# Level products of both head pairs in one run, a new order of the first loads, and three smaller moves

## The chip, the cores and the metric

The kernel runs on one core of a Trainium2 chip. The time is that of one execution on the device in microseconds (us), the median of several runs. One core has five engines with a queue of instructions each: TensorE (PE: matrix products; its weight loads are shown as PEld), VectorE (DVE), ScalarE (ACT), GpSimd (POOL) and SyncE (SP, which issues most loads). An engine works its queue in order; where an instruction needs something from another engine or from a DMA, it waits on a semaphore, and everything behind it waits too.

## The reference, cut to what matters

One layer of an encoder trunk with 512 rows (frames) of 1024 features, all float32:

```python
hn   = rmsnorm(x)
proj = hn @ w_in                      # fox q,k,v,f | hgrn q,f,i,g
A    = forgetting_attention(...)      # 8 heads of 64, causal softmax, bias F[t]-F[s]
B    = hgrn2_chunkwise(...)           # 4 heads, state 128x128, chunks of 64
x   += concat(A, B') @ w_out          # B' = rmsnorm(B) * silu(g)
x   += cross_attention(rmsnorm(x), rmsnorm(mem))   # 256 memory rows, 4 heads
x   += relu(rmsnorm(x) @ w1)**2 @ w2  # d_ff = 4096
out  = rmsnorm(x)
# inside hgrn2, for a chunk of 64 frames:
decay = exp(bcum[t] - bcum[s])        # for every feature d, s <= t
attn  = einsum('td,sd,tsd->ts', q, k, decay)
```

## The kernel before, in words

**Numbers.** Every product of projections is made with operands split into a high and a low part (fp32r), so one product of the reference is three on TensorE: high x high, high x low, low x high. `hn_hi`, `hn_lo` are the two parts of the normed input, `wh..` and `wl..` those of a weight panel. The high part is a copy on ScalarE (line 167), the low part a subtraction on VectorE (line 169), which needs the high part. A panel has 256 columns; number 11 has the halves `11a` and `11b` over K (the 1024 features that are summed over, in 8 chunks of 128).

**Order.** TensorE's instructions go in the order of the program text. The other engines' queues are ordered by a list scheduler with priorities when the kernel is built (`ahead(n)` shifts a priority, `tc.issue_after` and `tc.keep_in_program_order` bind one instruction behind others). `Fill` is a queue of generators of projection products: `fill.run(us)` takes steps from it until so many microseconds' worth have been issued. So TensorE has work between products whose operands are still being made.

**Start.** x is loaded by column blocks into `xt` (`load_x`): first columns 0 to 128 on SyncE's queue, then 128 to 256 and the next two blocks of 256 on ScalarE's, and the last on SyncE's behind the first weight panel, which is loaded in four parts of 256 KB (`load_next(4)`, `wr0a` twice and `wr0b` twice). `x_T(c)` transposes a chunk of 128 columns on TensorE into `xn`, `x_hi` and `x_lo` make `hn_hi`, `hn_lo` of it. Two accumulations `gf` (128 columns of the panel each) run over the eight chunks c, six products for each chunk, and `x_T(c + 2)` comes behind those of c. Before all of it, six products of zeros (`warm`) run.

**HGRN.** The decay between two frames in a chunk of 64 is split by levels: at level m = 1, 2, 4, .. 64 the frames are blocks of m, and the pairs in neighbouring blocks (odd block as t, even block as s) get their `attn` from one product of `mov` and `mix`. There are four heads in two head pairs (hp). For each level and each head pair: ScalarE copies `mix` from the scaled keys and queries; TensorE makes 16 small products of 64 x 64 into `lv` (8 of 128 x 128 at m = 64; line 670); VectorE copies them under a mask into `Ac` (`copy_predicated`, line 673); VectorE and GpSimd scale `sta` and `mov` (lines 693 and 694) by F, the decay to the edge of a block, and GpSimd brings F to the next level (line 696); then `fill.run(F2)`, 2.7 us of projections. The diagonal products `dg` (line 611), one for each of the four heads, with a `fill.run(F1)` of 1.6 us behind each, come ahead of the levels.

**Fox attention.** Units (head pair p, 128 rows tb, head j) are worked one behind another: bias, scores, a softmax (`mx` for the maximum, Exp, `dn` for the sum), and the transpose `pt` of the probabilities on TensorE, which is copied from PSUM into `pta`, `ptb` or `pts`, by ScalarE for j = 0 (line 910) and VectorE for j = 1 (line 912). Memory rows are transposed (`mnt`) in between, and split by ScalarE (`meh`) and VectorE (`mel`, line 365). Panels 11 and 12 (`wh11b`, `wl11b`, `wh12a`, ..) are split there too, for products that come later. `xq` and `k` operands (`q`, `kh`, `kl`) are made there.

**MLP.** It is computed in groups with sums of quadrants (a Strassen-like scheme): units of weights `whu`, `wlu` (up) and `whd`, `wld` (down); `prep` splits a unit's raw tile, `unit` calls `prep` for as many as four units ahead of use. `uU`, `uY` are products up, `c` and `h` are combined hidden parts, `hb` their high and low parts. A PSUM bank is free for the next product when VectorE or ScalarE has read it.

**Tail.** For each block of 128 rows, the squares of the last sum `acc` are added up in pieces (`squares`: ScalarE's Square with a sum, then `fe` adds the sum so far), GpSimd takes the power -1/2 (`fr`), and ScalarE and VectorE scale the rows (`fo`).

## Time and profile before

| what | value |
|---|---|
| median of 3 runs | 766.73 us (765.64 to 766.76) |
| the profiled execution | 765.97 us |
| its span, first to last instruction | 763.9 us |
| TensorE busy | 751.6 us (98%) |
| VectorE, ScalarE, GpSimd busy | 559.7, 427.1, 182.9 us |
| moved by DMA | 113.08 MB, 148 GB/s on average |

The span is shorter than the execution by 2.1 us, which lie around the first and the last instruction. In the rows below, a line of the timeline has the start, the duration, engine, line, what is written and read, the count, and in brackets the idle time ahead and what ended it; groups of equal instructions have one row. A line of the windows has the stretch, the sum, busy time and count by engine (PE, PEld, DVE, ACT, POOL, unless it is for certain instructions alone), TensorE's granted clock as a share of full speed, the share of the DMA engines' time and GB/s. A line of the waits has who waited for what: the total, the count and the longest.

### The profile page before, as it was taken

To read this page: it belongs to the slowest core of one execution; us is meant where nothing else is said; L and a number is where in the kernel's file an instruction comes from. 1 tells how busy PE (TensorE), PEld (TensorE's weight loads), DVE (VectorE), ACT (ScalarE), POOL (GpSimd) and SP (SyncE) were. 2 spreads that over 40 slices of the span, in tenths; PEclk is the share of its full clock that TensorE was granted. 3 is DMA by queue.
4 is the path that set the end of the run, shared out by engine and by line. 5 is a ranking of instruction groups with operands and counts; after the bars stand their busy time and mean duration, and the time that the engine had idled before them with its cause. 6 is when DMAs were issued, how large, how long until landed. Compare 5 with 4: busy or idle time off the path is not lost.

```text
span 763.9 us, 12648 instructions
## 1 busy us (share of the span) xinstructions
PE 751.6 (98%) x4844; PEld 665.8 (87%) x4844; DVE 559.7 (73%) x889; ACT 427.1 (56%) x718; POOL 182.9 (24%) x261
## 2 busy tenths in 40 slices
PE   8999999999999999999999999999999999999996
PEld 5889878978989988888888898999999999999985
DVE  4746766797677746645557789869797979897984
ACT  4655555676656533334445576656565757565743
POOL 7106343444343005510000111211212121211122
PEclk9999999999999999999999999999999999999998
DMA  7643322243444443221124498896979797978612
GB/s 225 216 114 86 111 82 57 84 111 85 142 161 137 131 150 111 87 79 56 56 83 137 83 295 171 231 253 161 249 165 241 183 268 164 280 148 213 161 47 110
DMA packets 84221, 113.08 MB, mean 148 GB/s; under 512 B 4881, under 2 KB 62778, under 8 KB 84162
## 3 DMA queue, kind: packets, MB, share of 16 engines
q1 hardware_dynamic: 70418, 74.77, 30.9%
q0 software_dynamic: 11568, 35.15, 22.6%
q10 hardware_dynamic: 2176, 2.36, 0.9%
q8 instruction: 38, 0.62, 0.3%
q14 instruction: 21, 0.17, 0.1%
HBM read 88.14 MB, written 4.21 MB: 121 GB/s over the span
## 4 chain that ended last, share of the span: by engine, by line
PE 90%; DVE 3%; DMA 2%; ACT 2%; issue 1%; POOL 1%; POOLq 0%; ACTq 0%; SPq 0%; DVEq 0%
PE uU L1394 4%; PE uU L1393 4%; PE uU L1395 4%; PE U L1495 3%; PE U L1496 3%; PE U L1497 3%; PE uY L1393 3%; PE uY L1395 3%; PE uY L1394 3%; PE xq L232 2%; PE xq L233 2%; PE xw L232 2%; PE xw L234 2%; PE xw L233 2%; PE xq L234 2%; PE wo L233 2%
## 5 line engine op out<-in xcount | busy, mean ns | idle before, releaser
L167 ACT ACTIVATE whd<-wq 128x1024 fp32r<-128x1024 f32 x39 | 41.3, 1058 | 31.3 <-PE U L1497 12.9
L169 DVE TENSOR_TENSOR wld<-wq,whd 128x1024 fp32r<-128x1024 f32 x39 | 47.6, 1220 | 7.1 <-ACT whd L167 7.1
L167 ACT ACTIVATE whu<-uq 128x1024 fp32r<-128x1024 f32 x28 | 29.7, 1062 | 33.0 <-PE uY L1394 14.3
L1395 PE MATMUL uU<-x2s,wlu 128*128 128x256 f32 x160 | 45.3, 283 | 0.0
L1393 PE MATMUL uU<-x2s,whu 128*128 128x256 f32 x160 | 45.2, 283 | 0.0
L1495 PE MATMUL U<-whd,hb 128*128 128x512 f32 x112 | 43.9, 392 | 0.0
L1496 PE MATMUL U<-wld,hb 128*128 128x512 f32 x112 | 43.9, 392 | 0.0
L1497 PE MATMUL U<-whd,hb 128*128 128x512 f32 x112 | 43.6, 389 | 0.0
L1250 POOL DMA_DIRECT2D uk<-us x8 | 7.2, 906 | 149.6 <-ACT acc L1114 85.7
L1467 DVE SCALAR_TENSOR_TENSOR acc<-U,r,acc 128x512 f32<-128x512 f32 x56 | 40.2, 744 | 1.8 <-PE U L1497 1.2
L169 DVE TENSOR_TENSOR wlu<-uq,whu 128x1024 fp32r<-128x1024 f32 x28 | 34.2, 1221 | 5.7 <-ACT whu L167 5.4
L1394 PE MATMUL uU<-x2a,whu 128*128 128x256 f32 x128 | 36.2, 283 | 0.0
L1394 PE MATMUL uY<-x2a,whu 128*128 128x256 f32 x128 | 36.2, 283 | 0.0
L1394 PE MATMUL uU<-x2b,whu 128*128 128x256 f32 x128 | 36.2, 283 | 0.0
L167 ACT ACTIVATE whu<-us 128x1024 fp32r<-128x1024 f32 x20 | 21.2, 1062 | 21.6 <-PE uU L1394 17.9
L169 DVE TENSOR_TENSOR wlu<-us,whu 128x1024 fp32r<-128x1024 f32 x20 | 24.4, 1221 | 10.8 <-ACT whu L167 10.8
L1393 PEld LDWEIGHTS uU<-x2s,whu 128*128 128x128 f32 x160 | 30.6, 191 | 0.8
L1395 PEld LDWEIGHTS uU<-x2s,wlu 128*128 128x128 f32 x160 | 30.6, 191 | 0.0
L889 ACT ACTIVATE bi<-bi,mx 128x128 f32<-128x128 f32 (+3 forms) x32 | 18.0, 561 | 20.5 <-DVE mx L887 20.2
L1250 POOL DMA_DIRECT2D wq<-in_w_dram x10 | 12.2, 1221 | 71.6 <-DMA wq<-in_w_dram 60.9
L872 POOL TENSOR_SCALAR bi<-nF,Ft 128x128 f32<-128x128 f32 (+3 forms) x32 | 21.5, 673 | 31.1 <-PE pt L899 17.1
L1393 PE MATMUL uY<-x2s,whu 128*128 128x256 f32 x96 | 27.3, 284 | 1.0 <-DVE c L1405 1.0
(961 smaller groups left out, 2809.1 us busy)
## 6 DMA issues: line engine op xcount, KB each, us to landing
wq<-in_w_dram SPq DMA_DIRECT2D x31, 512.0 KB, 6.0
uq<-in_w_dram SPq DMA_DIRECT2D x12, 512.0 KB, 4.7
us<-in_w_dram SPq DMA_DIRECT2D x12, 512.0 KB, 6.8
wq<-wq POOLq DMA_DIRECT2D x11, 512.0 KB, 6.4
wq<-in_w_dram POOLq DMA_DIRECT2D x10, 512.0 KB, 9.0
uk<-in_w_dram SPq DMA_DIRECT2D x8, 512.0 KB, 4.1
uk<-us POOLq DMA_DIRECT2D x8, 512.0 KB, 4.5
uq<-uk POOLq DMA_DIRECT2D x8, 512.0 KB, 6.1
```

What stands on the lines that cost most here:

```text
L167: ac.activation(hi, raw, AF.Copy)
L169: ve.tensor_tensor(lo, raw, f(hi), ALU.subtract)
L232: te.matmul(ps, wh, hi, start=n_ == 0, stop=False)
L233: te.matmul(ps, wh, lo, start=False, stop=False)
L234: te.matmul(ps, wl, hi, start=False, stop=n_ == KC - 1)
L1393: te.matmul(ps[:, i, :], whi[:, k, ws], xh, start=first_ and (k, i) == (0, 0), stop=False, skip_group_check=True)
L1394: te.matmul(ps[:, i, :], whi[:, k, ws], xl, start=False, stop=False, skip_group_check=True)
L1395: te.matmul(ps[:, i, :], wlo[:, k, ws], xh, start=False, stop=k == 3, skip_group_check=True)
L1467: ve.scalar_tensor_tensor(a, ps, r2[:, 0 if sign > 0 else 1, tb : tb + 1], a, op0=ALU.mult, op1=ALU.add)
L1495: te.matmul(ps, hi, whi[:, k, :], start=first_ and k == 0, stop=False, skip_group_check=True)
L1496: te.matmul(ps, hi, wlo[:, k, :], start=False, stop=False, skip_group_check=True)
L1497: te.matmul(ps, lo, whi[:, k, :], start=False, stop=k == 1, skip_group_check=True)
```

## The change

Five edits, which touch few instructions of TensorE.

1. *First loads and products.* SyncE now issues the columns of x from 256 on, between the parts of the first panel, and the first of these issues waits for a copy of one element on ScalarE (`xt<-ones`, behind ScalarE's table load), since it writes where the load writes. The first chunk's six products go high x high for both `gf`, then low weight, then `hn_lo`.
2. *Products in one run.* The `dg` products of a pair's two heads, and the `lv` products of both head pairs, follow each other, and the fill behind them is double. The scalings of `sta`, `mov` and F come, in the text, ahead of the copies under the mask.
3. *Two weights.* The split of the second half of panel 11 is put behind unit 3 of Fox attention, and the split of one MLP unit (u, 1, 6) behind the `hb` of part "6".
4. *Copies.* `pt` of the first head pair (p = 0) is copied by ScalarE for both heads.
5. *Last squares.* In the last block the last piece is squared on VectorE by one reduction that starts from the sum so far; the epsilon is added one step earlier.

```diff
@@ -152,7 +152,7 @@
     stream = []
-    state = {"used": 0, "then": None}
+    state, later = {"used": 0, "then": None}, []
     UW, UK = WT + FH, KC // 2
@@ -181,7 +181,9 @@
             for sl, src in spec:
-                nc.sync.dma_start(raw_[:, qs, sl], src[:, src_ks, :])
+                load = nc.sync.dma_start(raw_[:, qs, sl], src[:, src_ks, :])
+                if between is not None:
+                    tc.keep_in_program_order(load)
             if between is not None:
@@ -203,11 +205,14 @@
         while len(stream) < min(state["used"] + 2, len(specs)):
-            for split in load_next():
+            for half, split in enumerate(load_next()):
                 with ahead(PW), ExitStack() as order:
                         order.enter_context(tc.issue_after(ins))
-                    split()
+                    if (len(stream), half) == (12, 1):
+                        later.append(split)
+                    else:
+                        split()
         if state["used"] == len(specs) - 1:
@@ -222,16 +227,16 @@
-    def gemm_fm(ps, wt, col, ahi, alo, n=S, order=range(KC)):
+    def gemm_fm(ps, wt, col, ahi, alo, n=S, order=range(KC), begun=False):
             wh, wl = chunk(whi, k, sl), chunk(wlo, k, sl)
-            te.matmul(ps, wh, hi, start=n_ == 0, stop=False)
+            te.matmul(ps, wh, hi, start=n_ == 0 and not begun, stop=False)
             te.matmul(ps, wh, lo, start=False, stop=False)
-            te.matmul(ps, wl, hi, start=False, stop=n_ == KC - 1)
+            te.matmul(ps, wl, hi, start=False, stop=n_ == len(order) - 1)
             yield 3 * n / 2400
@@ -308,14 +313,19 @@
         gs = slice(g, g + n)
-        queue.dma_start(xt[:, :, gs], x[:, gs].rearrange("(t p) n -> p t n", p=P))
-
+        return queue.dma_start(xt[:, :, gs], x[:, gs].rearrange("(t p) n -> p t n", p=P))
+
+    ones = cp.tile([P, 1], F32, name="ones")
+    ve.memset(ones, 1.0)
     load_x(0, P, nc.sync)
     load_x(P, P)
-    for q in range(1, 3):
-        load_x(q * WT)
-    first = load_next(4)
-    load_x(3 * WT, queue=nc.sync)
+    tc.keep_in_program_order(ac.activation(xt[:, 0, WT : WT + 1], ones, AF.Copy))
+
+    def x_behind(part):
+        if part < 3:
+            tc.keep_in_program_order(load_x((part + 1) * WT, queue=nc.sync))
+
+    first = load_next(4, x_behind)
     rows = t2("rows", F32, (P,))[0:33, :]
@@ -330,8 +340,6 @@
     ve.memset(mhalf, -0.5)
-    ones = cp.tile([P, 1], F32, name="ones")
-    ve.memset(ones, 1.0)
@@ -444,7 +452,11 @@
         gfps = [mm(f"gf{i}") for i in range(2)]
-        gfg = [gemm_fm(gfps[i], wt0, i * P, hn_hi, hn_lo) for i in range(2)]
+        for part in ("hh", "lh", "hl"):
+            for i, ps in enumerate(gfps):
+                w, a = (wt0["hl".index(part[0])][0][:, 0, i * P : (i + 1) * P], (hn_hi, hn_lo)["hl".index(part[1])][:, 0, :])
+                te.matmul(ps, w, a, start=part == "hh", stop=False)
+        gfg = [gemm_fm(gfps[i], wt0, i * P, hn_hi, hn_lo, order=range(1, KC), begun=True) for i in range(2)]
         second = []
@@ -471,7 +483,7 @@
         for c in range(KC):
-            for g in gfg:
+            for g in gfg if c else ():
                 next(g)
@@ -611,7 +623,7 @@
             gp.tensor_tensor(qt_(h), qt_(h), Fg[hp][:, j, :], op=ALU.mult)
-            fill.run(F1)
+        fill.run(2 * F1)
@@ -655,8 +667,9 @@
             gate_rows()
+        lvs = []
         for hp in range(2):
-            F_, M_, S_ = Fg[hp], Mv[hp], Sa[hp]
+            M_ = Mv[hp]
             mix = t2(f"mix{hp}{m}", F32, (NT, P))
@@ -664,10 +677,21 @@
             ps = sc(f"lv{hp}{m}", (NT, 2, w))
+            lvs.append(ps)
             for c in range(NT):
                     te.matmul(ps[o : o + 2 * w, c].rearrange("p u (b m) -> p u b m", m=m), mix[:, c, o : o + 2 * w], rhs, start=True, stop=True)
+        for hp in range(2):
+            F_, ps = Fg[hp], lvs[hp]
+            for j in range(2):
+                h = 2 * hp + j
+                qv, kv, fv = halves(qt_(h), m), halves(kt_(h), m), halves(F_[:, j, :], m)
+                bshape = [P, S // (2 * m), m]
+                ve.tensor_tensor(qv[:, :, 1, :], qv[:, :, 1, :], fv[:, :, 0, 0:1].to_broadcast(bshape), ALU.mult)
+                (ve, gp)[j].tensor_tensor(kv[:, :, 0, :], kv[:, :, 0, :], fv[:, :, 1, 0:1].to_broadcast(bshape), op=ALU.mult)
+            fv = halves(F_.rearrange("p h t -> p (h t)"), m)
+            gp.tensor_tensor(fv[:, :, 0, 0:1], fv[:, :, 0, 0:1], fv[:, :, 1, 0:1], op=ALU.mult)
             if m < 64:
@@ -686,15 +710,7 @@
                     last_copy.append(ve.tensor_copy(A_[hi_, 4:8, lo_], ps[hi_, :, 1, :]).ins)
-            for j in range(2):
-                h = 2 * hp + j
-                qv, kv, fv = halves(qt_(h), m), halves(kt_(h), m), halves(F_[:, j, :], m)
-                bshape = [P, S // (2 * m), m]
-                ve.tensor_tensor(qv[:, :, 1, :], qv[:, :, 1, :], fv[:, :, 0, 0:1].to_broadcast(bshape), ALU.mult)
-                (ve, gp)[j].tensor_tensor(kv[:, :, 0, :], kv[:, :, 0, :], fv[:, :, 1, 0:1].to_broadcast(bshape), op=ALU.mult)
-            fv = halves(F_.rearrange("p h t -> p (h t)"), m)
-            gp.tensor_tensor(fv[:, :, 0, 0:1], fv[:, :, 0, 0:1], fv[:, :, 1, 0:1], op=ALU.mult)
-            fill.run(F2)
+        fill.run(2 * F2)
     fq, fk = {}, {}
@@ -861,7 +877,7 @@
     units = [(p, tb, j) for p in range(4) for tb in range(NT) for j in range(2)]
-    prob, probT, held_T = {}, {}, {}
+    prob, probT, held_T, ends = {}, {}, {}, {}
@@ -886,9 +902,9 @@
             den = sm(1, f"dn{h}{tb}")
-            ac.activation(b, b, AF.Exp, bias=mx, scale=-1.0, accum_out=den)
+            exp = ac.activation(b, b, AF.Exp, bias=mx, scale=-1.0, accum_out=den)
             ve.reciprocal(den, den)
-            ve.tensor_scalar(b, b, den, None, op0=ALU.mult)
+            ends[u] = exp.ins, ve.tensor_scalar(b, b, den, None, op0=ALU.mult).ins
@@ -906,7 +922,7 @@
                 probT[u] = held_T[p, tb % 2][:, j, (0 if tb else 3 * P) :][:, 0:n]
-            if j == 0:
+            if j == 0 or p == 0:
                 ac.activation(probT[u], pt[:, 0:n], AF.Copy)
@@ -957,6 +973,9 @@
                 fill.until("fv0")
+            if n == 4:
+                with ahead(PW), tc.issue_after(ends[units[3]][0]), tc.issue_after(ends[units[3]][1]):
+                    later.pop()()
             if n + 1 < len(units):
@@ -1279,7 +1298,7 @@
-    last_sum = {}
+    last_sum, hb_ins = {}, {}
@@ -1311,7 +1330,7 @@
         unit_ = new_parts([k, D // k], f"{kind}{g}{name}")
-        with ahead(PW):
+        with ahead(PW), tc.issue_after(hb_ins[0, "6"]) if (kind, g, name) == ("u", 1, "6") else nullcontext():
             split_of(unit_[0], unit_[1], raw.rearrange("p (k n) -> p k n", k=k))()
@@ -1323,7 +1342,8 @@
         kept = sum(k in units and keys.index(k) < keys.index(key) for k in last_keys)
-        while unit_q and kept + sum(k in units for k in keys[keys.index(key) :]) < 4:
+        room = 3 if key == ("u", 1, "2") else 4
+        while unit_q and kept + sum(k in units for k in keys[keys.index(key) :]) < room:
             prep(*unit_q.popleft())
@@ -1431,7 +1451,7 @@
         sign = -1.0 if name == "6" else 1.0
-        ac.activation(hb[:, 0], src, AF.Copy, scale=sign)
+        hb_ins[g, name] = ac.activation(hb[:, 0], src, AF.Copy, scale=sign).ins
         if name == "6":
@@ -1515,10 +1535,15 @@
             outs[tb] = k4([D], f"fo{tb}")
+        if last and tb == NT - 1:
+            a = acc[tb][:, cs]
+            tc.keep_in_program_order(ve.tensor_tensor_reduce(out=outs[tb][:, cs], in0=a, in1=a, scale=1.0 / D, scalar=sums[tb][-1], op0=ALU.mult, op1=ALU.add, accum_out=ms))
+            sums[tb].append(ms)
+            return
         ac.activation(outs[tb][:, cs], acc[tb][:, cs], AF.Square, scale=1.0 / 32.0, accum_out=ms)
             e = sm(1, f"fe{tb}{n}")
-            (ve if last else gp).tensor_scalar(e, ms, sums[tb][-1], EPS if last else 0.0, op0=ALU.add, op1=ALU.add)
+            (ve if last else gp).tensor_scalar(e, ms, sums[tb][-1], EPS if last or tb == NT - 1 else 0.0, op0=ALU.add, op1=ALU.add)
             ms = e
```

SyncE's queue at the program's start, before (xt: the columns of x; wr0a, wr0b: the first panel's raw halves; rows: the small gains):

```order
L311 DMA xt<-in_x_dram 128x4x128
L184 DMA wr0a<-in_w_in_dram 128x2x256 x2
L184 DMA wr0b<-in_w_in_dram 128x2x256 x2
L311 DMA xt<-in_x_dram 128x4x256
L321 DMA rows<-in_norm_x_g_dram 8x128
L321 DMA rows<-in_norm_mem_g_dram 8x128
L321 DMA rows<-in_norm_ff_g_dram 8x128
L322 DMA rows<-in_hgrn_norm_g_dram 1x128
L323 DMA rows<-in_hgrn_lb_logits_dram 8x128
```

and now:

```order
L316 DMA xt<-in_x_dram 128x4x128
L184 DMA wr0a<-in_w_in_dram 128x2x256
L331 DMA rows<-in_norm_x_g_dram 8x128
L331 DMA rows<-in_norm_mem_g_dram 8x128
L331 DMA rows<-in_norm_ff_g_dram 8x128
L316 DMA xt<-in_x_dram 128x4x256
L184 DMA wr0a<-in_w_in_dram 128x2x256
L316 DMA xt<-in_x_dram 128x4x256
L184 DMA wr0b<-in_w_in_dram 128x2x256
L316 DMA xt<-in_x_dram 128x4x256
L184 DMA wr0b<-in_w_in_dram 128x2x256
L332 DMA rows<-in_hgrn_norm_g_dram 1x128
```

The columns of x from 256 on have moved into this queue, between the panel's parts; three of the rows' loads stand ahead of them.

TensorE in the first level, before (lv: the level's products, gi: the projections that fill), around the first head pair's products:

```order
L246 MATMUL gi_717<-wl4a,hn_hi 128x264
L247 MATMUL gi_717<-wh4a,hn_lo 128x264
L670 MATMUL lv_737<-mov_408,mix_734 64x64 x8
L245 MATMUL gi_717<-wh4b,hn_hi 128x264
L246 MATMUL gi_717<-wl4b,hn_hi 128x264
```

and around the second's, behind 24 rows of gi:

```order
L246 MATMUL gi_767<-wl4a,hn_hi 128x264
L247 MATMUL gi_767<-wh4a,hn_lo 128x264
L670 MATMUL lv_783<-mov_411,mix_780 64x64 x8
L245 MATMUL gi_767<-wh4b,hn_hi 128x264
L246 MATMUL gi_767<-wl4b,hn_hi 128x264
```

and now:

```order
L251 MATMUL gi_718<-wl4a,hn_hi 128x264
L252 MATMUL gi_718<-wh4a,hn_lo 128x264
L684 MATMUL lv_738<-mov_409,mix_735 64x64 x8
L684 MATMUL lv_750<-mov_412,mix_747 64x64 x8
L250 MATMUL gi_718<-wh4b,hn_hi 128x264
L251 MATMUL gi_718<-wl4b,hn_hi 128x264
```

Both head pairs' products now follow each other, with one change from gi to lv and one back; 48 rows of gi stand behind them.

ScalarE in the MLP, at the second half of the first group (whu: high half of an up unit's weight, n and s: sums of hidden parts, whose high part is hb, uU: up products), before:

```order
L1434 ACTIVATE hb_4982<-sq_4715 128x512
L167 ACTIVATE whu_5013<-uq_4597 128x1024
L167 ACTIVATE whu_5045<-uq_4596 128x1024
L1434 ACTIVATE hb_5010<-n_0_5007 128x512
L1398 ACTIVATE h_5043<-uU_5018 128x512
L1434 ACTIVATE hb_5101<-s_0_5006 128x512
L167 ACTIVATE whd_5079<-wq 128x1024
```

and now:

```order
L1454 ACTIVATE hb_4983<-sq_4716 128x512
L167 ACTIVATE whu_5014<-uq_4598 128x1024
L1418 ACTIVATE h_5044<-uU_5019 128x512
L1454 ACTIVATE hb_5011<-n_0_5008 128x512
L1454 ACTIVATE hb_5102<-s_0_5007 128x512
L167 ACTIVATE whu_5075<-uq_4597 128x1024
L167 ACTIVATE whd_5080<-wq 128x1024
```

The second whu has moved behind h and two hb.

## The prediction

> **What bounds the kernel now.** I read the page first (busy shares, clock row), then the waits of TensorE (PE), since an engine that is nearly always busy can lose time only in its waits, its clock or its own switching.
>
> ```profile
> PE 751.6 (98%) x4844; PEld 665.8 (87%) x4844; DVE 559.7 (73%) x889; ACT 427.1 (56%) x718; POOL 182.9 (24%) x261
> PEclk9999999999999999999999999999999999999998
> PE xn L405 <- DMA xt<-in_x_dram: 1.8, 1, 1.8
> PE uY L1393 <- DVE c L1405: 1.0, 1, 1.0
> PE pt L899 <- DVE mel L365: 0.5, 1, 0.5
> PE mnt L362 <- DVE ptb L912: 0.4, 1, 0.4
> ```
>
> PE works for 751.6 of 763.9 us: 12.3 us are idle. The last four rows are its waits inside the program that the change can reach; they make 3.7 us. Vector (73%), Scalar (56%) and GpSimd (24%) matter only where PE stands waiting for them. So each part of the change is priced by what PE does at that place, and what makes a product shorter or a switch rarer counts in full.
>
> **The start.** The chain, the timeline and windows of 2 us:
>
> ```profile
> 1.45 5.64 DMA xt<-in_x_dram
> 3.01 1.28 ACT L167 ACT_TABLE_LOAD   x1 [3.01 <-issue]
> 6.39 0.67 ACT L408 ACTIVATE hn_hi<-xn,g_mix 128x512 fp32r<-128x512 f32 x1
> 7.13 0.66 PE L405 MATMUL xn<-ident,xt 128*128 128x128 f32 x4 [1.79 <-DMA xt<-in_x_dram]
> 7.54 0.47 PE L232 MATMUL gf<-hn_hi,wh0a 128*128 128x512 f32 x1
> 13.01 0.47 PE L232 MATMUL gf<-hn_hi,wh0a 128*128 128x512 f32 x1
> 4.00:6.00 2.00, 1.24 (x6) 0.89 (x5) 0.17 (x1) 0.43 (x2) 2.00 (x8) 1.00 1.06 333
> 6.00:8.00 2.00, 0.87 (x6) 0.65 (x6) 1.35 (x2) 1.24 (x3) 2.00 (x5) 1.00 1.09 377
> 8.00:10.00 2.00, 2.00 (x7) 1.25 (x7) 0.75 (x1) 0.51 (x1) 2.00 (x7) 0.63 1.09 384
> 10.00:12.00 2.00, 2.00 (x8) 1.72 (x8) 0.34 (x1) 1.06 (x2) 2.00 (x9) 0.52 0.76 263
> ```
>
> The second 128 columns of x, issued at 1.45, land at 7.09, because everything is issued at once and shares 333 to 384 GB/s (the windows' last column). PE waits 1.79 us for them, starts its first product at 7.54, and then runs at a granted clock of 0.63 and 0.52 for 4 us (the column before the last two): 2 x (1 - 0.63) / 0.5 + 2 x (1 - 0.52) / 0.5 = 3.4 us at half speed, which costs 1.7 us. At 13.01 the third chunk of K begins.
>
> After, only 768 KB (two column blocks of x, the first weights) stand ahead of the dummy activation; the rest of x is behind it. The table load moves up from 3.01, behind two issues instead of four, to about 2, so the next columns of x are issued at about 3.6. At the windows' 333 KB in a us, and with the first bytes moving at about 2.7 (an estimate: the issue at 1.45 and somewhat over 1 us), they are in by 5.0, with stragglers 5.3. Then the weight's high half (0.6), hn_hi (0.67): the first product at 6.6. Six products, 0.23 apart as the same ones are later at full clock, end at 8.0. The four products that need only hn_hi come first now, so the two with hn_lo find it done at 7.4 (0.74 on Vector behind hn_hi). The next columns (512 KB, with 256 KB of weights, at 377 KB in a us) are in by 7.4, ahead of their use at 8.0. Transposes of 0.45, six products, transposes: third chunk at 10.3, if the clock stays full. That is 2.7 earlier than 13.01. PE would be idle for some 0.7 us between 5 and 8.5 instead of over 2, and I see no reason for the clock to fall. If it still falls for 3.4 us, 1.7 go back: 1.0. Upper end 2.8. I take 2.4, near the upper end, with 0.3 off for stragglers, since the landing of 7.09 was one of these. The first loads of rows on SyncE's queue are 4 KB each and now stand ahead of x's next columns, issued in 0.3 us each, by 3.3, before the activation releases those: no cost. PE itself issues the same count of instructions.
>
> **Products in runs.** PE leaves a run of projections for 16 small products and returns. Timeline, and windows that count the small products alone:
>
> ```profile
> 67.50 0.28 PE L246 MATMUL gi<-wl4a,hn_hi 128*128 128x264 f32 x1
> 67.61 0.28 PE L247 MATMUL gi<-wh4a,hn_lo 128*128 128x264 f32 x1
> 67.83 0.69 PE L670 MATMUL lv<-mov,mix 128*64 128x64 f32 x16
> 68.45 0.39 PE L245 MATMUL gi<-wh4b,hn_hi 128*128 128x264 f32 x1
> 68.67 0.28 PE L246 MATMUL gi<-wl4b,hn_hi 128*128 128x264 f32 x1
> 67.83:68.06 0.23, 0.23 (x8) 1.00 0.00 0
> 67.83:68.30 0.47, 0.47 (x16) 1.00 0.00 0
> 71.53 0.28 PE L670 MATMUL lv<-mov,mix 128*64 128x64 f32 x2
> ```
>
> Projections start 0.115 us apart. The first small product comes 0.22 after the last projection: 0.10 lost. 16 products start within 0.47, yet the next projection starts at 0.62 after the first: 0.15 lost. The second projection comes 0.22 behind the first: 0.10 lost. One excursion thus costs 0.35. The change merges two into one at two places of the diagonal products and six of the level products with 64 columns: 8 x 0.34 = 2.7. The seventh level has products of 128 x 128, for which no such row stands here: 0 to 0.1, taken as 0. Bounds: nothing but the second projection's 0.10 saved, 0.8; all of 0.35 and 0.1 on the last, 2.9. I take 2.7, because the rows measure the very instructions.
>
> The cover for it: behind the products, Vector and GpSimd scale and mask for the next level.
>
> ```profile
> 67.82 0.43 DVE L693 TENSOR_TENSOR sta<-sta,F 128x256 f32<-128x256 f32 x1 [0.61 <-ACT mix L664]
> 68.56 0.76 DVE L673 COPY_PREDICATED Ac<-mku,lv 128x128 f32<-128x128 uint8 x2 [0.31 <-PE lv L670]
> 69.11 0.64 DVE L693 TENSOR_TENSOR mov<-mov,F 128x256 f32<-128x256 f32 x1
> 68.61 0.86 POOL L694 TENSOR_TENSOR mov<-mov,F 128x256 f32<-128x256 f32 x1 [1.28 <-PE lv L670]
> 70.26 1.04 POOL L696 TENSOR_TENSOR F<-F 128x512 f32<-128x512 f32 x1 [0.79 <-DVE mov L693]
> ```
>
> Runs of one head pair came 3.70 apart (67.83, 71.53); two of them give 7.4 less the 0.35, and of this 6.1 is filling. Vector needs for both pairs 4 x 0.43 + 2 x 0.64 + 2 x 0.76 = 4.5, of which the four scalings of sta wait for no product of PE; with one low half of a weight (1.22) 5.7. GpSimd needs 2 x (0.86 + 1.04) = 3.8. Both fit into 6.1, by 0.4 and 2.3. The scalings ahead of the masked copies put the F updates and the next mix first. No new wait, cost 0; bound 1.5 in all.
>
> **The two weights and the copies.** Timeline in Fox attention:
>
> ```profile
> 156.39 1.38 DVE L169 TENSOR_TENSOR wl11b<-wr11b,wh11b 128x1024 fp32r<-128x1024 f32 x1
> 164.01 0.47 ACT L364 ACTIVATE meh<-mnt,gv 128x256 fp32r<-128x256 f32 x1
> 166.52 1.22 DVE L169 TENSOR_TENSOR wl12a<-wr12a,wh12a 128x1024 fp32r<-128x1024 f32 x1
> 167.73 0.40 DVE L912 COPY ptb<-pt 128x256 f32<-128x256 f32 x1
> ```
>
> PE's wait at pt (0.5, above) is for mel, which stood behind wl11b on Vector until 157.77. With wl11b gone from there, mel is done before PE asks: 0.5 and the restart of 0.1, 0.6 saved. The wait at mnt (0.4) is for a bank that ptb empties, on Vector behind wl12a at 167.73 to 168.13. Now Scalar copies it, and in its queue stand, behind the meh that ends at 164.48, the moved wh11b (1.06, as whu in the next fence), a copy (0.4), wh12a (1.06), an exponential (0.6), a meh (0.47): 164.48 + 1.06 + 0.4 + 1.06 + 0.6 + 0.47 + 0.4 = 168.5. So it ends some 0.3 later than before, and PE comes 0.6 earlier by the first wait's loss: the first wait's 0.6 is partly given back, 0.3. Net 0.3. Bounds: the second wait gone too, 1.1 (0.6 + 0.5); or the copy late by a weight's 1.06 more, -0.7, since wl11b now also stands ahead of wl12a on Vector (the first's 1.22 and the second's in a row), and the load that reuses its buffer starts later, with kh behind it on Scalar.
>
> The MLP's weight, by the timeline:
>
> ```profile
> 466.32 1.06 ACT L167 ACTIVATE whu<-uq 128x1024 fp32r<-128x1024 f32 x1 [4.20 <-DMA uq<-uk]
> 468.54 1.22 DVE L169 TENSOR_TENSOR wlu<-uq,whu 128x1024 fp32r<-128x1024 f32 x1
> 469.68 0.68 DVE L1405 TENSOR_TENSOR c<-uY,h 128x512 f32<-128x512 f32 x1
> ```
>
> Scalar stands for 4.20 us until a load lands, and behind it stand the two instructions that c needs. c runs at 469.68, 1.0 after PE wanted its bank. After, h and the two hb copies go first; c can run by about 468.2, and PE wants it at 469.3: the wait of 1.0 is gone, and its restart of 0.1. whu itself ends at about 469.2 and its low half by 471.3; the products that use it begin 0.9 later in the order. Bounds 0 (the low half is late for its own products by what was saved) and 1.1; I take 1.0.
>
> **The last squares.** Timeline of the tail:
>
> ```profile
> 757.23 0.42 ACT L1518 ACTIVATE fo<-acc 128x256 f32<-128x256 f32 x1 [0.86 <-DVE acc L1467]
> 757.84 0.21 DVE L1521 TENSOR_SCALAR fe<-fm,fe 128x1 f32<-128x1 f32 x1 [0.65 <-ACT fo L1518]
> 758.14 0.99 POOL L1544 TENSOR_TENSOR fr<-fe,mhalf 128x1 f32<-128x1 f32 x1 [0.89 <-DVE fe L1521]
> 159.40 0.41 DVE L887 CUSTOM_DVE_ANT_0 bi<-ps,bi 128x256 f32<-128x256 f32 x1
> ```
>
> From the square's start to fr are 0.91 us over two changes of engine. One reduction on Vector of the last row's kind (0.41, its read of the sum 0.08) starts at once behind acc: fr at about 757.85, 0.3 earlier; bounds 0 and 0.4. I take 0.3.
>
> **The sum.** 2.4 + 2.7 + 0.3 + 1.0 + 0.3 = 6.7 us. The profiled execution took 765.97 (span 763.9 and 2.1 around it), so 759.3. It stands 0.8 below the median of the runs (766.73), and inside their scatter of 1.1; half of that goes on top: 759.6.
>
> **Rivals.**
> - *The clock falls anyway at the start.* For: it stood at 0.52 to 0.63 right after the idle stretch, and PE will still wait for hn_hi there. Against: the idle part is a third of what it was. Then the start brings 1.0 less 0.1, and the time is 759.6 + 1.5 = 761.1. [...]
> - *Scalar becomes what PE waits for in attention.* For: three splits (3.2 us) and two copies in a row there. Against: the page has Scalar at 56%. The copy late by a weight: 1.0 worse than taken, 760.6; copies early throughout: 0.8 better, 758.8.
> - *The loads don't come earlier.* That is the change not doing what it says: the columns of x behind the activation starve the second or third chunk, and the gated queue gives back what the first landing gained. Start 0, time 762.0.
> - *Slower: the level chain becomes the bound.* Each level's last masked copy or scaled mov now ends behind two head pairs' work on one queue, and the next run of products needs it. For: Vector's 5.7 of 6.1 us in the estimate, and two low halves in one gap make 6.9. Against: GpSimd has 2.3 to spare and the scalings stand ahead of the copies. To lose, 6.7 + 1.5 must go in seven gaps: 1.2 us of wait in each, so Vector's queue would have to reach 7.3 in every one. At 1.3 each the time is 768.7. Waits of 0.3 each, which is likelier, cost 2: 761.6.
>
> **Chances.** The forecast 0.56; the clock 0.18; Scalar in attention 0.08 (and 0.05 early copies, inside the range); loads 0.05; short waits in the levels 0.04; slower 0.04. Some 0.2% (1.5 us) is what this kernel's measurement tells from no change. Faster by more than that: all cases but the last and some of the loads' and small pieces, 0.92; within it 0.04; slower 0.04. Range: from 757.0 (the upper bounds of start, attention and products, 0.4 + 0.8 + 0.2, and the runs' scatter of 1.1) to 763.0 (the loads' case and the same scatter).
>
> **What would show it.** In the profile after: the first wait row (xn for x) shorter than 0.5 and PE's clock at 1.00 between 8 and 12; gf's third chunk at about 10.3; level products as groups of 32 about 1.1 us long with 7 us between them and no row of waits that names lv or mix; the rows for uY and pt gone, mnt's between 0.3 and 1; fr in the tail following a Vector reduction. It is wrong if PE's waits gain rows for lv, mix or dg, if the clock row of the start still has the half stretch, or if pt and mnt merely change their releaser to Scalar with more time.

## The result, and the profile after

The changed kernel takes 758.62 us (median of 4 runs, 758.36 to 758.67); beside it the kernel before took 766.18 (4 runs, 765.36 to 766.76). The ratio is 0.9901, with a 95% interval of 0.9884 to 0.9919: 7.6 us faster, where 759.6 (757.0 to 763.0) was forecast. The profiled execution took 758.36, with a span of 756.5.

From the page after, TensorE's row, and behind it from its waits the rows that answer to those of before (total, count, longest in us):

```profile
PE 746.6 (99%) x4844; PEld 663.9 (88%) x4844; DVE 558.3 (74%) x886; ACT 428.0 (57%) x721; POOL 191.0 (25%) x261
```

```profile
PE xn L413 <- DMA xt<-in_x_dram: 0.7, 1, 0.7
PE lv L684 <- issue: 0.5, 1, 0.5
```

The rows for uY, pt and mnt are gone, that for x went from 1.8 to 0.7, and a row for lv is new. Idle time of TensorE fell from 12.3 to 9.9 us and its busy time from 751.6 to 746.6: more of the gain lies in products that became shorter or closer than in waits.

To see where the 7.4 us of the span come from, the starts of the same product in both traces are set against each other, along the program. The difference changes at few places (in brackets, from the second row on, the difference ahead of the place and behind it, where products follow at their usual distance again):

| place | gain there, us | forecast |
|---|---|---|
| start, up to the third chunk's first product (13.01 to 9.90) | 3.1, some 0.15 of it given back by the panel's end (2.96 remain) | 2.4 |
| eight merged runs of small products (2.96 to 5.77) | 2.8 | 2.7 |
| last level's products (5.77 to 5.03) | -0.7 | 0 |
| Fox attention, pt and mnt (5.03 to 6.08) | 1.05 | 0.3 |
| MLP, uY (6.08 to 7.29) | 1.2 | 1.0 |
| tail (7.29 to 7.47) | 0.2 | 0.3 |

Timeline of the start, and its windows:

```profile
5.62 0.66 PE L413 MATMUL xn<-ident,xt 128*128 128x128 f32 x4 [0.69 <-DMA xt<-in_x_dram]
...
6.23 0.72 PE L458 MATMUL gf<-hn_hi,wh0a 128*128 128x512 f32 x2
...
9.90 0.48 PE L237 MATMUL gf<-hn_hi,wh0a 128*128 128x512 f32 x1
```

```profile
8.00:10.00 2.00, 2.00 (x14) 1.69 (x13) 0.92 (x2) 1.21 (x2) 2.00 (x6) 1.00 1.05 362
10.00:12.00 2.00, 2.00 (x13) 1.47 (x12) 1.52 (x3) 1.70 (x3) 2.00 (x7) 1.00 1.07 341
```

The second 128 columns land at 5.6 instead of 7.1, and the windows that had a granted clock of 0.63 and 0.52 now have 1.00, with 14 and 13 matrix instructions instead of 7 and 8.

Timeline at the first level's products:

```profile
63.95 0.28 PE L252 MATMUL gi<-wh4a,hn_lo 128*128 128x264 f32 x1
64.16 1.16 PE L684 MATMUL lv<-mov,mix 128*64 128x64 f32 x32
65.25 0.39 PE L250 MATMUL gi<-wh4b,hn_hi 128*128 128x264 f32 x1
65.48 0.29 PE L251 MATMUL gi<-wl4b,hn_hi 128*128 128x264 f32 x1
```

32 products take 1.09 up to the next projection, where two runs of 16 took 0.62 each, and the 0.10 on either side (63.95 to 64.16, 65.25 to 65.48) are paid once: 0.15 + 0.20 = 0.35 a merge.

Timeline of TensorE, then of ScalarE, ahead of the last level's products:

```profile
107.81 0.60 PE L654 MATMUL pFr<-ident,Ft 128*8 128x128 f32 x4
108.92 2.02 PE L684 MATMUL lv<-mov,mix 128*128 128x128 f32 x16 [0.51 <-issue]
```

```profile
107.15 1.06 ACT L167 ACTIVATE wh9a<-wr9a 128x1024 fp32r<-128x1024 f32 x1 [1.19 <-PE gg L238]
108.11 0.40 ACT L676 ACTIVATE mix<-sta 128x256 f32<-128x256 f32 x1
108.42 0.40 ACT L677 ACTIVATE mix<-sta 128x256 f32<-128x256 f32 x1
...
109.03 0.40 ACT L677 ACTIVATE mix<-sta 128x256 f32<-128x256 f32 x1
```

Four transposes of 0.11 begin at 107.81, so TensorE could go on at 108.25 and does at 108.92. The four mix copies (the third is left out) stand here behind a weight's high half; the two of the first head pair end at 108.82. The wait has no named releaser ("issue"). Before, the products followed the transposes at once, and the weight's high half came behind the last mix copy, as the chain that ended last (start, duration, name, count) and ScalarE's timeline show:

```profile
113.75 0.44 PE pFr L642 x4
114.19 0.89 PE lv L670 x8
```

```profile
113.62 0.40 ACT L664 ACTIVATE mix<-sta 128x256 f32<-128x256 f32 x1
113.92 1.04 ACT L167 ACTIVATE wh9a<-wr9a 128x1024 fp32r<-128x1024 f32 x1
```

Timeline in Fox attention (ScalarE, TensorE), in the MLP (ScalarE, VectorE), and of the tail:

```profile
158.42 1.05 ACT L167 ACTIVATE wh11b<-wr11b 128x1024 fp32r<-128x1024 f32 x1
...
161.68 0.38 ACT L926 ACTIVATE ptb<-pt 128x256 f32<-128x256 f32 x1
...
162.12 0.44 PE L370 MATMUL mnt<-ident,mt 128*128 128x128 f32 x2
```

```profile
461.02 1.06 ACT L167 ACTIVATE whu<-uq 128x1024 fp32r<-128x1024 f32 x1 [1.30 <-DMA uq<-uk]
...
461.33 0.68 DVE L1425 TENSOR_TENSOR c<-uY,h 128x512 f32<-128x512 f32 x1
```

```profile
749.42 0.48 DVE L1487 SCALAR_TENSOR_TENSOR acc<-y,r,acc 128x256 f32<-128x256 f32 x1 [0.17 <-PE y L1529]
...
750.09 0.49 DVE L1540 CUSTOM_DVE_ANT_0 fo<-acc,fe 128x256 f32<-128x256 f32 x1 [0.19 <-POOL fe L1546]
...
750.67 1.00 POOL L1569 TENSOR_TENSOR fr<-fm,mhalf 128x1 f32<-128x1 f32 x1 [0.61 <-DVE fm L1540]
```

ptb is copied by 162.06, and mnt starts at 162.12 with no wait row. whu still stands for its load, but c (461.33) no longer stands behind it. In the tail, from the start of the last acc to fr are 1.25 us, before 1.43 (756.71 to 758.14), from this row of the timeline before:

```profile
756.71 0.48 DVE L1467 SCALAR_TENSOR_TENSOR acc<-y,r,acc 128x256 f32<-128x256 f32 x1 [0.17 <-PE y L1509]
```

### The profile page after: what moved, and what is told of

The parts are those of the page before. It is cut to its first block, busy times and chain, and to the rows that moved or that the text cites. A ratio compares the mean times of both kernels' runs of the same rounds, so it can differ in the third digit from the quotient of the medians.

```text
span 756.5 us, 12647 instructions
## 1 busy us (share of the span) xinstructions
PE 746.6 (99%) x4844; PEld 663.9 (88%) x4844; DVE 558.3 (74%) x886; ACT 428.0 (57%) x721; POOL 191.0 (25%) x261
## 4 chain that ended last, share of the span: by engine, by line
PE 98%; DMA 1%; issue 0%; DVE 0%; POOL 0%; POOLq 0%; ACTq 0%; ACT 0%
PE uU L1415 4%; PE uU L1414 4%; PE uU L1413 4%; PE U L1515 3%; PE U L1516 3%; PE U L1517 3%; PE uY L1415 3%; PE uY L1414 3%; PE uY L1413 3%; PE xq L237 2%; PE xq L238 2%; PE xw L237 2%; PE xw L239 2%; PE xw L238 2%; PE xq L239 2%; PE wo L237 2%
## 5 line engine op out<-in xcount | busy, mean ns | idle before, releaser
L888 POOL TENSOR_SCALAR bi<-nF,Ft 128x128 f32<-128x128 f32 (+3 forms) x32 | 25.0, 783 | 29.1 <-PE pt L915 17.2
```

## Experiments

**How to read the times.** The end of the half clock at the program's start differs between traces of kernels that are the same up to there, by about 1.5 us of time (third chunk at 9.90 and at 11.39); it is told below. The medians are also from different rounds: the kernel before took 766.18 us beside the changed kernel, but 764.91 to 765.56 beside the experiments, and the changed kernel was not run again. So medians of different kernels compare to 1 or 2 us, and a part's effect is read from the trace, as the difference between the starts of the same products behind the start.

**Merged runs alone** (the kernel before with edit 2).

```diff
# in the levels of the kernel before, and dg alike
-        for hp in range(2): mix; lv products; masked copies; scalings; fill.run(F2)
+        for hp in range(2): mix; lv products
+        for hp in range(2): scalings; masked copies
+        fill.run(2 * F2)
```

> The kernel before with edit 2 alone (dg and lv products in one run, doubled fill, scalings ahead of the masked copies). Theory A: each of the eight merges saves one change between projections and small products, 0.35 us by the rows of the profile before, 2.8 in all, and the last level then waits about 0.7 for its mix copies, because the split of panel 9 has come to stand ahead of them on ScalarE: 2.1 us faster, about 764.1. Theory B: the wait of the last level in the changed kernel belongs to the earlier start (everything on ScalarE arrives sooner relative to its loads), not to the merged runs: 2.8 us faster, about 763.4, and no wait ahead of the products of 128 x 128.

763.10 us (6 runs, 762.51 to 763.46), before 765.56 (17 runs): ratio 0.9962 (0.9947 to 0.9977). In the trace the gain grows by 0.33 to 0.38 at each of the eight merges, from 0.79 to 3.60, and then falls to 2.86 at the last level. Its waits:

```profile
PE uY L1397 <- DVE c L1409: 1.4, 1, 1.4
PE pt L903 <- DVE mel L365: 0.6, 1, 0.6
PE lv L672 <- issue: 0.5, 1, 0.5
PE mnt L362 <- DVE ptb L916: 0.4, 1, 0.4
```

Theory A holds: the last level's wait comes with the merge, not with the earlier start. Of the merges 2.1 us remain behind the last wait. The wait for c grows from 1.0 to 1.4: the products come 2.9 earlier, the weight's high half that c stands behind only 2.4 (463.93 for 466.32).

**Panel 9's split behind the mix copies.**

```diff
-                    for ins in last_copy[-2:] if len(stream) == 10 else ():
+                    for ins in last_copy[-4:] if len(stream) == 10 else ():
```

> The changed kernel, with the split of panel 9 bound behind the last four noted instructions instead of two, which puts wh9a behind the four mix copies of the last level on ScalarE. Theory A: the idle time of TensorE ahead of the last level's products (start to start 0.78 where 0.11 is usual) is made by wh9a (1.06 us on ScalarE) standing ahead of the copies; it goes, 0.5 to 0.7 us faster than the changed kernel's 758.62, about 758.0. Theory B: these products wait for GpSimd's scaling of F or for the transposes of the gate sums ahead of them; then nothing changes, 758.6.

759.24 us (5 runs, 758.93 to 760.02), ratio 0.9914 (0.9898 to 0.9931). Timeline of TensorE, then of ScalarE, at the last level:

```profile
109.34 0.60 PE L654 MATMUL pFr<-ident,Ft 128*8 128x128 f32 x4
109.78 1.95 PE L684 MATMUL lv<-mov,mix 128*128 128x128 f32 x16
```

```profile
108.32 0.40 ACT L677 ACTIVATE mix<-sta 128x256 f32<-128x256 f32 x1
108.67 1.06 ACT L167 ACTIVATE wh9a<-wr9a 128x1024 fp32r<-128x1024 f32 x1
```

The products follow the transposes at once (0.44), and 0.76 us are won there against the changed kernel: theory A by the trace. How it came about is in the code: the split is bound behind the last two entries of a list of copies. Before, these were the second pair's mix copy and a copy on VectorE; in the new order of the text they are two copies on VectorE, so nothing holds wh9a behind the mix copies on ScalarE. The time isn't better than 758.62 all the same, because the half clock at the start was longer, at least in the profiled run (the others have no trace), as the timeline and a window of its start show:

```profile
6.36 1.20 PE L458 MATMUL gf<-hn_hi,wh0a 128*128 128x512 f32 x2
7.36 1.05 PE L458 MATMUL gf<-hn_hi,wl0a 128*128 128x512 f32 x2
8.22 1.05 PE L458 MATMUL gf<-hn_lo,wh0a 128*128 128x512 f32 x2
```

```profile
6.00:8.00 2.00, 2.00 (x8) 1.71 (x7) 1.60 (x3) 0.86 (x2) 2.00 (x5) 1.00 0.98 294
```

The same products have 0.72, 0.63 and 0.62 in the changed kernel's trace. The window beside them states a granted clock of 1.00: the clock column doesn't show the half speed of the start, the products' distance does (0.43 here, 0.23 there). In this trace the third chunk starts 1.5 later than in the changed kernel's.

**Old order of loads.** The changed kernel with the loads of before; the first six products stay in their new order.

```diff
     load_x(P, P)
-    tc.keep_in_program_order(ac.activation(xt[:, 0, WT : WT + 1], ones, AF.Copy))
-    first = load_next(4, x_behind)
+    for q in range(1, 3):
+        load_x(q * WT)
+    first = load_next(4)
+    load_x(3 * WT, queue=nc.sync)
```

> The changed kernel with the loads in the order of before (x from 256 columns on in ScalarE's queue, no dummy activation), but the first chunk's six products in their new order. Theory A: nearly all of the 3.0 us that the start gained come from the loads, by the earlier landing of the second 128 columns and the clock that then stays full: 2.5 to 3.0 slower than the changed kernel, about 761.3, with granted clock near 0.5 between 8.5 and 12 us. Theory B: a good part comes from the order of the first six products: under 2 us slower, below 760.6.

760.33 us (6 runs, 759.83 to 761.19), ratio 0.9927 (0.9912 to 0.9942). Timeline:

```profile
6.54 0.66 PE L410 MATMUL xn<-ident,xt 128*128 128x128 f32 x4 [1.09 <-DMA xt<-in_x_dram]
...
9.08 0.66 PE L410 MATMUL xn<-ident,xt 128*128 128x128 f32 x4 [0.48 <-DMA xt<-in_x_dram]
...
11.32 0.48 PE L237 MATMUL gf<-hn_hi,wh0a 128*128 128x512 f32 x1
```

The third chunk starts 1.4 later than in the changed kernel, and 1.8 are lost to the end; in the medians 1.7. It is theory B's number: under 2. But the rest of the 3.1 isn't all the order of the products. In this execution the clock didn't fall between 8.5 and 12 (1.00 in the windows, products 0.23 apart), although TensorE idled 1.1 us ahead of it, and x landed at 6.5, not 7.1.

**The idle stretch filled** (the kernel before, with products of zeros in it).

```diff
         x_T(0)
+        warm2 = pvt("warm2")
+        for _ in range(7):
+            te.matmul(warm2, zero[:, 0:P], zero, start=True, stop=True)
         x_T(1)
```

> The kernel before, with seven products of zeros behind the first four transposes, where TensorE stood idle for 1.8 us; the loads stay as they were. They write a scratch bank that nobody reads. Theory A: the half clock from 8.5 to 12 us was made by the idle stretch ahead of it; with the stretch filled the clock stays full there and the third chunk begins at about 11.7 instead of 13.0: 1.0 to 1.4 us faster, about 765.0. [...]

764.90 us (12 runs, 763.68 to 766.90), ratio 0.9989 (0.9977 to 1.0001). Timeline:

```profile
5.24 2.03 PE L440 MATMUL warm<-zero 128*128 128x512 bf16 x7
...
7.47 0.48 PE L232 MATMUL gf<-hn_hi,wh0a 128*128 128x512 f32 x1
...
11.19 0.48 PE L232 MATMUL gf<-hn_hi,wh0a 128*128 128x512 f32 x1
```

In the profiled run the clock stays full (1.00 in the windows from 4 to 14, products 0.23 apart) and the third chunk starts 1.8 earlier than in the profile before, with the loads as they were; to the end 1.5 remain. So of the 3.1 us between the profiles before and after, about 1.8 are the fall of the clock in the first, and 1.3 the loads and the order of the first products. The medians differ by 0.7 alone, and the interval takes in no change. The mean granted clock is 0.995, as in the profile with the fall, in 4 of the 17 runs of before beside it, and in 1 of these 12. So by this measure the fall was in that profile and in about a quarter of the runs, not in all. It doesn't sort the times by itself: among the runs of before, one with 0.995 took 765.27 us and one with 0.997 took 767.34. The profile agrees with theory A; 4 of 17 against 1 of 12 is too little to show that the zeros prevent the fall in general.

**Order of the first six products.**

```diff
-        for part in ("hh", "lh", "hl"):
-            for i, ps in enumerate(gfps):
+        for i, ps in enumerate(gfps):
+            for part in ("hh", "hl", "lh"):
```

> The changed kernel with the first chunk's six products in the old order (all three of one accumulation, then the other). Theory A: the low part of the input is ready about 0.85 us after TensorE's first product, and the second product needs it: where the clock is full by then, 0.3 to 0.5 slower, read off the trace between the first product and the first transposes of the third chunk; where the clock is half, the products themselves take long enough, and it costs under 0.2. Theory B: the next transposes wait for their load, which hides it: nothing at either clock.

759.96 us (4 runs, 759.15 to 760.49), ratio 0.9934 (0.9920 to 0.9948). Timeline:

```profile
6.22 0.49 PE L458 MATMUL gf<-hn_hi,wh0a 128*128 128x512 f32 x1
7.01 0.50 PE L458 MATMUL gf<-hn_lo,wh0a 128*128 128x512 f32 x1 [0.29 <-DVE hn_lo L419]
```

TensorE waits for the low part, and the transposes of the third chunk come 2.06 behind the first product (at 8.28), in the changed kernel 1.49 (at 7.72): 0.57 lost. Both traces are at full clock there (products 0.23 apart); it is a little more than theory A's 0.3 to 0.5, and the loads don't hide it. So of the start's 3.1 us some 0.6 belong to this order. Another 0.36 is lost at 543 us, in the MLP; its cause is open.

**The two edits in Fox attention**, each undone in the changed kernel, and both.

```diff
# the split of panel 11's second half at its old place
-                    if (len(stream), half) == (12, 1):
+                    if False:
# (and its new place behind unit 3 taken out)
# the copies back on VectorE
-            if j == 0 or p == 0:
+            if j == 0:
```

> The changed kernel with the split of panel 11's second half at its old place. Theory A: mel stands behind wl11b on VectorE again and TensorE waits for it at pt, 0.6 to 0.8 us more, counted in the trace from the first to the last product, so that the start's clock doesn't enter. Theory B: the copies on ScalarE alone opened that wait's bank soon enough, and the move of the weight did nothing: under 0.2.

> The changed kernel with the four copies of pt for the second head of the first pair back on VectorE. Theory A: the copy stands behind wl11b and wl12a, which now follow each other on VectorE until 162.2, and TensorE, which needs its bank at mnt from about 161.8, waits 0.6 to 0.9 us there instead of the 0.28 lost now: 0.4 to 0.6 slower in the trace. Theory B: the copies only moved work, the mnt wait is made by the weight's split on either engine: within 0.2.

> The changed kernel with both edits in Fox attention undone (the split of panel 11's second half at its old place, the copies back on VectorE). Theory A: the two edits belong together: undoing the copies alone left two weights' low halves ahead of a copy on VectorE and cost about 2 us there; with both undone it is the state of before, waits at pt and mnt of 0.5 and 0.4, 1.1 slower than the changed kernel between the first pt and the last mnt. Theory B: they add up: 0.75 and 2.0 make 2.7.

The split put back: 759.56 us (4 runs); 0.97 lost at pt and just behind it, 0.22 regained at a later mnt, 0.75 in all: theory A. The copies put back: 760.53 us (4 runs); 0.39 and 1.53 lost at two mnt, 1.9 together: more than either theory. Both: 761.41 us (4 runs, 759.34 to 761.47); 1.0 lost from the first pt to the last mnt: theory A. VectorE and TensorE with the copies alone put back, by the timeline, and the waits with both put back:

```profile
163.61 1.21 DVE L169 TENSOR_TENSOR wl12a<-wr12a,wh12a 128x1024 fp32r<-128x1024 f32 x1
...
165.61 0.41 DVE L928 COPY ptb<-pt 128x256 f32<-128x256 f32 x1
...
166.17 0.41 PE L370 MATMUL mnt<-ident,mt 128*128 128x128 f32 x2 [1.67 <-DVE ptb L928]
```

```profile
PE pt L915 <- DVE mel L373: 0.6, 1, 0.6
...
PE mnt L370 <- DVE ptb L928: 0.4, 1, 0.4
```

The edits don't add up. With the weight's low half moved and the copy on VectorE, the copy stands behind two low halves and steps of a softmax, and TensorE waits 1.7: the move of the weight would have cost 0.9 us by itself (1.9 less 1.0), and needs the move of the copies. I had expected 0.4 to 0.6 for it: I counted the two weights, not the softmax's steps that stand between them and the copy.

**The MLP's weight, and the last squares**, undone.

```diff
-        with ahead(PW), tc.issue_after(hb_ins[0, "6"]) if (kind, g, name) == ("u", 1, "6") else nullcontext():
+        with ahead(PW):
-        room = 3 if key == ("u", 1, "2") else 4
+        room = 4
# the last squares: Square on ScalarE and the sum on VectorE, as in the kernel before
```

> The changed kernel with the split of the MLP's unit (u, 1, 6) at its old place. Theory A: ScalarE stands until that unit's load lands, c comes late, and TensorE waits at uY again: 1.0 to 1.2 us slower in the trace, all of it there. Theory B: with the rest of the kernel some 6 us earlier the load is later against the products, so the wait is longer than before: 1.3 to 1.6.

> The changed kernel with the last block's last piece squared on ScalarE and added on VectorE as before. Theory A: from the last acc to fr the chain takes 1.43 us again instead of 1.25, 0.18 us slower in the span, too little for the times. Theory B: what the reduction on VectorE saves is 0.3, as the prediction had it, and GpSimd's sum that it waits for was only late in that one trace.

The weight at its old place: 760.67 us (5 runs, 759.92 to 762.91); in the trace 1.46 at uY, and nothing elsewhere:

```profile
PE uY L1413 <- DVE c L1425: 1.2, 1, 1.2
```

It is theory B's number, and its reason is in the trace: the weight's high half that c stands behind starts 5.8 earlier than in the kernel before (460.48 for 466.32), the products 6.1 earlier. The squares on ScalarE: 760.84 us (4 runs); the span behind TensorE's last products grows by 0.15, and from acc (750.91) to fr (752.34) are 1.43 again: theory A, and nothing that these times can tell.

**Scalings behind the masked copies.**

```diff
# in the levels of the changed kernel
         for hp in range(2):
-            scalings of sta, mov and F
             masked copies
+        for hp in range(2):
+            scalings of sta, mov and F
         fill.run(2 * F2)
```

> The changed kernel with the scalings of sta, mov and F behind the masked copies of both head pairs, as they stood for one pair before; the products stay in one run. Theory A: each gap between two runs of products has about 6 us of projections, and VectorE with GpSimd needs less in either order, so TensorE waits nowhere that it doesn't now: within 0.2 in the trace behind the start. Theory B (the slower rival of the prediction): with the scalings last, the next mix is late, and TensorE waits ahead of several runs, 0.3 to 1 us each, 1 to 5 slower.

759.25 us (4 runs, 758.15 to 760.55), ratio 0.9931 (0.9916 to 0.9947); in the trace no difference above 0.15 behind the first products, and its one wait in the levels is that of the last. Theory A. The order of scalings and copies in the text makes no difference; the slower rival was far off.

**Both mended: the mix copies first, and eight products of zeros at the start.**

```diff
-WARM = 6
+WARM = 8
-                    for ins in last_copy[-2:] if len(stream) == 10 else ():
+                    for ins in last_copy[-4:] if len(stream) == 10 else ():
```

> The changed kernel with panel 9's split behind the last mix copies, and eight products of zeros at the start instead of six. [...]

758.58 us (5 runs, 758.17 to 759.84), ratio 0.9918 (0.9906 to 0.9931). The last level's wait is gone, 0.76 won there. In the profiled run the clock is full when the input's products begin (0.23 apart), but these come later, because the transposes stand behind the zeros:

```profile
5.18 1.68 PE L413 MATMUL xn<-ident,xt 128*128 128x128 f32 x8
7.08 0.73 PE L458 MATMUL gf<-hn_hi,wh0a 128*128 128x512 f32 x2 [0.21 <-ACT hn_hi L416]
```

6.23 became 7.08: the zeros cost 0.85 against the changed kernel's trace. Against the trace with the long half clock they gain 0.6 (third chunk at 10.75, there 11.39). One run of five lies at 759.84, the others at 758.17 to 758.66, so the scatter is not gone. This isn't shown to beat the changed kernel; the mended order of the copies alone, worth 0.76 by the trace, is the part to keep.

## Why the prediction was right, point by point

- *The start: mis-sized.* 2.4 was taken with an upper end of 2.8; the traces give 3.1. What came in as foreseen: the landing (5.3 forecast, 5.58 in the trace; for the somewhat over 1 us from an issue to its first bytes, the profile before has its first issue at 0.80 and a DMA share of 0.00 up to 1.7 and 0.25 by 2.0) and the full clock between 8 and 12; the wait for x is still 0.7, where a row under 0.5 was to show the step. The first product came at 6.23, not 6.6, since the weight's high half started at 4.96. The order of the six products was reckoned as keeping the low part from being waited for, but given no number; it is worth 0.6 at full clock. The rest is partly luck of the two profiles: the clock's fall, worth 1.8, was in the profile before and by the mean clock in a quarter of the runs, the profile after has the early end of the half clock at the start, which moves the third chunk by 1.5, and the loads undone cost 1.7. My rival "the clock falls anyway" named the right quantity. What decides when the half clock ends, no run shows.
- *Products in runs: right in step and size.* 0.33 to 0.37 a merge, eight merges, 2.8 for 2.7. That Vector's and GpSimd's work fits the gaps held, with room: even with the scalings last no run of 64 columns waited.
- *"No new wait, cost 0": failed at the last level.* A row of waits for lv was one of the prediction's own signs of being wrong, and it is there. The cover that I priced was Vector's and GpSimd's queue; what came late was ScalarE's, by a weight that the new order no longer held back. 0.7 lost, within the bound of 1.5 that stood there. ScalarE's queue at this place wasn't read in the prediction.
- *Fox attention: mis-sized, 0.3 for 1.05.* The first wait went nearly as forecast (0.77 with its restart, for 0.6). The step that failed is the second: "the copy ends 0.3 later, and PE comes 0.6 earlier". I moved TensorE ahead by the first wait's 0.6 but left ScalarE's chain where it was, though it moves with TensorE: the meh at its head starts 5.97 earlier than before (158.04 for 164.01), TensorE's mnt ahead of it 6.04 earlier (157.25 for 163.29). From the end of that meh to the end of the copy I had 4.0 us; the trace has 3.6 (158.51 to 162.06). Both together make the copy ready as TensorE comes.
- *The MLP: right.* 1.0 forecast, 1.2 in the trace, 1.46 when undone.
- *The tail: half.* 0.3 forecast, 0.18 from acc to fr: the reduction waited 0.19 for GpSimd's sum of the piece before, whose end (757.25 in the chain of before) was not taken into the step.
- *The slower rival.* It needed Vector's queue at 7.3 us in each gap. No level but the last has a wait, and that one is ScalarE's.

The sum came out near because errors had both signs: +0.55 at the start (2.96 for 2.4), +0.1 in the merged runs, +0.75 in Fox attention and +0.2 in the MLP, against -0.75 at the last level and -0.1 in the tail. Some luck is likely in the measured time too: the four runs of the changed kernel lie within 0.3 us, near the fastest runs (758.15 and 758.60) of the kernel with the scalings last, which equals it behind the start but whose other two runs took 759.90 and 760.55.

## What to carry to other kernels

On a kernel whose bound is an engine that is 98% busy, count its changes of shape: each excursion of TensorE into small products of 64 columns cost 0.35 us here, for the diagonal products and the levels' alike, and merging two saved that much where nobody had to wait. When a step moves, shift with it everything that it feeds, and read every queue past which it moves, those of the copies too; two moves can pay together where one alone is worth little or costs time (undone, the weight's move cost 0.75, the copies' 1.9, and both only 1.0). An order that is bound to "the last two of a list" changes its meaning when the text is reordered.

## What was not expected of the hardware

The half clock at the program's start doesn't end at a fixed time. By the distance of like products (products of 512 columns are 0.23 us apart at full clock, 0.43 at half), it ended near 4.4 us in the changed kernel's profile and near 9 in that of the kernel with the mix copies first, with the same instructions up to there; the third chunk started at 9.90 and at 11.39. Neither is an exception: of the ten traces with the new loads, five have that start at 9.70 to 10.75, and five at 11.37 to 11.93. The profile's clock column reads 1.00 throughout both. What decides it wasn't settled; with eight products of zeros, up to 4.9 us, one run in five was still over 1 us above the others. The landing of x's second block with the old loads also moved: its transposes start at 5.70, 6.54, 7.11 and 7.13 in the four traces, with the new loads and six products of zeros at 5.51 to 5.76 in all nine. In these traces the new order of loads made the landing steadier, and not only earlier. For gains below 2 us in this kernel, two profiles have to be compared behind the start, product by product.
